# Issuing the first slab's store as two DMAs, the first in 4 KB and the second in 28 KB descriptors

One core of a Trainium2 (trn2) chip. The metric is the device time of one execution in microseconds (us).

## The reference

Rotary position embedding with heads split: `x` is 16 x 512 x 1024 float32 (33.55 MB), the output has the same size, and the two tables are small.

```python
x = x.reshape(batch, seq, num_heads, head_dim)
x1, x2 = x[..., :half_dim], x[..., half_dim:]
rotated = np.concatenate([x1 * cos - x2 * sin,
                          x1 * sin + x2 * cos], axis=-1)
```

## The kernel before

`x` is handled in 8 slabs of 4 MB, each as 128 partitions x 8 rows x 1024 elements; a partition's 32 KB are contiguous in DRAM. There are five slab buffers (`slots`), so load 5 has to wait for store 0, load 6 for store 1 and load 7 for store 2. Loads are issued on SP, stores on ACT. ACT casts a slab to bf16, DVE does two multiplications and an addition, and ACT casts back into the slab. The first slab and the last two are done in two halves of four rows.

```python
def load(s):
    slab[s] = slabs.tile([P, W], f32, tag="slab", name="slab")
    return nc.sync.dma_start(out=slab[s], in_=dram(x, s))
...
for s in range(nslabs):
    n = rpp if 1 <= s < nslabs - 2 else rpp // 2
    passes += [(s, r, n) for r in range(0, rpp, n)]

cast(passes[0])
for i, (s, r, n) in enumerate(passes):
    if i + 1 < len(passes):
        cast(passes[i + 1])
    ...                                    # two tensor_mul, one tensor_add on DVE
    nc.scalar.copy(out=xs, in_=xu)
    if r + n == rpp:
        nc.scalar.dma_start(out=dram(out_flat, s), in_=slab[s])
        if s + slots < nslabs:
            load(s + slots)
```

Of the kernel before, what the change touches and what calls it, by code (L numbers as in the profile page):

```python
# [2 lines left out]

# [4 lines left out]


@with_exitstack  # L10
def kernel(
    ctx: ExitStack,
    tc: tile.TileContext,
    x: bass.AP,
    cos: bass.AP,
    sin: bass.AP,
    num_heads: int,
    out: bass.AP,
):
    nc = tc.nc  # L20
    P = nc.NUM_PARTITIONS

    batch, seq, dim = x.shape
    nh = num_heads
    hd = dim // nh
    half = hd // 2
    bf16 = mybir.dt.bfloat16
    f32 = mybir.dt.float32

    nb = 2  # L30
    slots = 5
    nslabs = batch // nb
    rpp = nb * seq // P
    W = rpp * dim
    SP = seq // rpp
    TW = rpp * half

    out_flat = out.rearrange("b s h d -> b s (h d)")

    singles = ctx.enter_context(tc.tile_pool(name="singles", bufs=1))  # L40
    slabs = ctx.enter_context(tc.tile_pool(name="slabs", bufs=slots))
    xpool = ctx.enter_context(tc.tile_pool(name="xpool", bufs=2))
    psum = ctx.enter_context(tc.tile_pool(
        name="psum", bufs=1, space=bass.MemoryType.PSUM))


    def dram(t, s, a=0, n=W):
        return bass.AP(tensor=t.tensor, offset=t.offset + s * nb * seq * dim + a,
                       ap=[[W, P], [1, n]])


    def view(t, offset, *dims):
        return dataclasses.replace(t, offset=t.offset + offset,
                                   ap=[t.ap[0], *[list(d) for d in dims]])


    slab = {}
# [7 lines that stand above are left out]
    load(0)  # L65


    TR = seq // P
    G = rpp // TR
    table = {}  # L70
    raw = singles.tile([P, 2 * TR * half], f32, tag="raw")
    for i, src in enumerate((cos, sin)):
        table[i] = nc.gpsimd.dma_start(out=view(raw, i * TR * half, (1, TR * half)), in_=bass.AP(  # L73
            tensor=src.tensor, offset=src.offset,
            ap=[[TR * half, P], [1, TR * half]]))



    for s in range(1, slots):
        tc.add_manual_dep(  # L80
            load(s).ins, table[0].ins.name,
            mybir.DependencyInfo(mybir.DependencyClass.Sync,
                                 mybir.DependencyReason.DATA),
            reason="issue")



    pick = singles.tile([P, 2 * G * P], bf16, tag="pick")
    nc.gpsimd.memset(pick, 0.0)  # L89
    for g in range(2 * G):  # L90
        part = view(pick, g * P, (SP, P // SP), (1, SP))
        nc.gpsimd.affine_select(  # L92
            out=part, in_=part, compare_op=mybir.AluOpType.not_equal,
            fill=1.0 if g < G else -1.0, base=-(g % G),
            pattern=[[0, P // SP], [-G, SP]], channel_multiplier=1)

    tab1 = singles.tile([P, 2 * TR * half], bf16, tag="tab1")
    nc.gpsimd.tensor_copy(out=tab1, in_=raw)  # L98

    acc = psum.tile([P, 2 * rpp * hd], f32, tag="acc")  # L100
    for i in range(2):
        for h in range(2):
            for g in range(G):
                nc.tensor.matmul(  # L104
                    view(acc, (i * rpp + g * TR) * hd + h * half, (hd, TR), (1, half)),
                    view(pick, (i * h * G + g) * P, (1, P)),
                    view(tab1, i * TR * half, (half, TR), (1, half)),
                    start=True, stop=True)
    tab = singles.tile([P, 2 * rpp * hd], bf16, tag="tab")
    nc.vector.tensor_copy(out=tab, in_=acc)  # L110

    xb = {}


    def cast(u):
        s, r, n = u
        if r == 0:
            xb[s] = xpool.tile([P, W], bf16, tag="xb", name="xb")
        nc.scalar.copy(out=view(xb[s], r * dim, (1, n * dim)),  # L119
                       in_=view(slab[s], r * dim, (1, n * dim)))  # L120




    passes = []
# [9 lines that stand above are left out]
        xs = view(slab[s], r * dim, (1, n * dim))  # L135
        xu = view(xb[s], r * dim, (1, n * dim))

        t2 = view(slab[s].bitcast(bf16), 2 * r * dim, (1, n * dim))
        for t, a in ((t2, rpp * hd), (xu, 0)):
            nc.vector.tensor_mul(  # L140
                out=t, in0=xu,
                in1=view(tab, a + r * hd, (hd, n), (0, nh), (1, hd)))
        nc.vector.tensor_add(  # L143
            out=xu, in0=xu, in1=view(t2, half, (hd, n * nh), (-half, 2), (1, half)))

        nc.scalar.copy(out=xs, in_=xu)  # L146
        if r + n == rpp:
            nc.scalar.dma_start(out=dram(out_flat, s), in_=slab[s])
            if s + slots < nslabs:
                load(s + slots)  # L150


# [1 line left out]
_INS = ['x', 'cos', 'sin', 'num_heads']  # L154
_OUTS = [((16, 512, 16, 64), 'float32')]

_NUMBERS = {'num_heads': 16}


# [26 lines left out]
```

## Time and profile before

| | before |
|---|---|
| time, first chip, median of 4 runs | 162.02 us (161.98 to 162.12) |
| span of the profiled run | 160.4 us |
| bytes moved, mean rate | 67.24 MB, 419 GB/s |
| busiest compute engine | ACT, 71% |
| last store issued, landed | 145.28, 14.2 us later |

The page's own lines stand in the prediction below, with how to read them. In short: the DMA engines are full nearly all the time and no other engine is. One line more, from the view of the loads (minimum, median and maximum of the time from issue to landing); the maximum is load 4:

```profile
DMA to landing us min/median/max: 12.6/24.5/55.3
```

### The profile page before, as it was taken

The page shows a single profiled execution, that of the slowest core. Times are in us where ns is not written, and L with a number is a line of the kernel's source. Part 1 is how long each engine was busy: PE and PEld are TensorE (multiplying, and loading weights), DVE is VectorE, ACT ScalarE, POOL GpSimd, SP SyncE. Part 2 cuts the span into 40 slices and gives each one's busy share as a digit, 9 for nine tenths or more (in the row PEclk, how much of TensorE's full clock was granted, in tenths as well). Part 3 has the DMA queues.
Part 4 walks back from the last instruction along what each step waited for, and adds up shares of the span by engine and source line. Part 5 has one row for each costly group of instructions (what it writes and reads, how often), then busy time and mean ns, then how long its engine had stood idle before and what let it go on. Part 6 is the DMA issues. An engine that isn't in the chain of part 4 may idle for free.

```text
span 160.4 us, 169 instructions
## 1 busy us (share of the span) xinstructions
PE 1.0 (1%) x8; PEld 0.8 (1%) x8; DVE 108.5 (68%) x34; ACT 113.5 (71%) x23; POOL 3.4 (2%) x12
## 2 busy tenths in 40 slices
PE   0011000000000000000000000000000000000000
PEld 0010000000000000000000000000000000000000
DVE  0003799999989979997996099939749599930000
ACT  3006939998998999899907997099995999462000
POOL 7000000000000000000000000000000000000000
DMA  7999999999999999999999999999999999999995
GB/s 245 425 409 409 474 425 400 466 441 392 384 400 400 507 400 400 466 441 392 441 474 392 433 482 392 425 482 400 400 507 400 400 474 433 392 449 466 392 433 221
DMA packets 2368, 67.24 MB, mean 419 GB/s; under 512 B 288, under 2 KB 288, under 8 KB 320
## 3 DMA queue, kind: packets, MB, share of 16 engines
q1 hardware_dynamic: 1152, 33.55, 49.5%
q10 hardware_dynamic: 1152, 33.55, 48.4%
q0 software_dynamic: 64, 0.13, 0.2%
HBM read 33.69 MB, written 33.55 MB: 419 GB/s over the span
## 4 chain that ended last, share of the span: by engine, by line
DMA 59%; ACT 17%; issue 9%; DVE 4%; SPq 0%; ACTq 0%; POOLq 0%
DMA slab<-in_x_dram 39%; DMA out_dram<-slab 15%; ACT slab L146 11%; ACT xb L119 6%; DMA raw<-in_cos_dram 4%; DVE xb L140 1%; DVE xb L143 1%; DVE slab L140 1%; SPq L62 0%; ACTq L146 0%; POOLq L167 0%
## 5 line engine op out<-in xcount | busy, mean ns | idle before, releaser
L119 ACT CAST xb<-slab 128x4096 bf16<-128x4096 f32 (+1 forms) x11 | 56.6, 5155 | 27.5 <-DMA slab<-in_x_dram 26.2
L146 ACT CAST slab<-xb 128x4096 f32<-128x4096 bf16 (+1 forms) x11 | 56.6, 5153 | 3.5 <-DVE xb L143 3.5
L140 DVE TENSOR_TENSOR slab<-xb,tab 128x4096 bf16<-128x4096 bf16 (+1 forms) x11 | 35.9, 3260 | 19.9 <-ACT xb L119 19.8
L140 DVE TENSOR_TENSOR xb<-xb,tab 128x4096 bf16<-128x4096 bf16 (+1 forms) x11 | 35.9, 3261 | 0.3
L143 DVE TENSOR_TENSOR xb<-xb,slab 128x4096 bf16<-128x4096 bf16 (+1 forms) x11 | 35.9, 3261 | 0.3
L110 DVE CAST tab<-acc 128x1024 bf16<-128x1024 f32 x1 | 1.2, 1225 | 12.5 <-PE acc L104 12.5
L119 ACT ACT_TABLE_LOAD x1 | 1.3, 1283 | 0.7 <-PEq L167 0.7
L104 PE MATMUL acc<-tab,pick 128*128 128x128 bf16 x8 | 1.0, 305 | 11.5 <-POOL tab L98 11.5
L92 POOL TENSOR_SCALAR_AFFINE_SELECT pick<-pick 128x128 bf16<-128x128 bf16 x4 | 1.0, 288 | 0.1
L104 PEld LDWEIGHTS <-pick 128*128 128x128 bf16 x8 | 0.8, 136 | 11.4 <-issue 8.0
L73 POOL DMA_DIRECT2D raw<-in_cos_dram x1 | 0.7, 674 | 0.8 <-POOLq L167 0.8
L89 POOL MEMSET pick<- 128x512 bf16 x1 | 0.5, 543 | 0.0
L98 POOL CAST tab<-raw 128x256 bf16<-128x256 f32 x1 | 0.4, 396 | 6.9 <-DMA raw<-in_sin_dram 6.9
L73 POOL DMA_DIRECT2D raw<-in_sin_dram x1 | 0.5, 534 | 0.0
L167 POOL MEMSET const-float32-0.0<- 128x1 f32 x1 | 0.1, 99 | 0.2 <-issue 0.2
L167 POOL MEMSET const-bfloat16-1.0<- 128x1 bf16 x1 | 0.1, 102 | 0.0
L167 POOL MEMSET const-uint8-127<- 128x1 uint8 x1 | 0.1, 102 | 0.0
L167 POOL MEMSET const-float32-1.0<- 128x1 f32 x1 | 0.1, 99 | 0.0
## 6 DMA issues: line engine op xcount, KB each, us to landing
slab<-in_x_dram SPq DMA_DIRECT2D x8, 4096.0 KB, 24.5
out_dram<-slab ACTq DMA_DIRECT2D x8, 4096.0 KB, 26.6
raw<-in_cos_dram POOLq DMA_DIRECT2D x1, 64.0 KB, 7.0
raw<-in_sin_dram POOLq DMA_DIRECT2D x1, 64.0 KB, 9.0
```

Source lines behind the costliest of these rows:

```text
L73: table[i] = nc.gpsimd.dma_start(out=view(raw, i * TR * half, (1, TR * half)), in_=bass.AP(tensor=src.tensor, offset=src.offset, ap=[[TR * ...
L89: nc.gpsimd.memset(pick, 0.0)
L92: nc.gpsimd.affine_select(out=part, in_=part, compare_op=mybir.AluOpType.not_equal, fill=1.0 if g < G else -1.0, base=-(g % G), pattern=[[ ...
L98: nc.gpsimd.tensor_copy(out=tab1, in_=raw)
L104: nc.tensor.matmul(view(acc, (i * rpp + g * TR) * hd + h * half, (hd, TR), (1, half)), view(pick, (i * h * G + g) * P, (1, P)), view(tab1, ...
L110: nc.vector.tensor_copy(out=tab, in_=acc)
L119: nc.scalar.copy(out=view(xb[s], r * dim, (1, n * dim)), in_=view(slab[s], r * dim, (1, n * dim)))
L140: nc.vector.tensor_mul(out=t, in0=xu, in1=view(tab, a + r * hd, (hd, n), (0, nh), (1, hd)))
L143: nc.vector.tensor_add(out=xu, in0=xu, in1=view(t2, half, (hd, n * nh), (-half, 2), (1, half)))
L146: nc.scalar.copy(out=xs, in_=xu)
L167: nc = _bacc.Bacc("TRN2", target_bir_lowering=False, num_devices=1)
```

## The change

Its form suggests an intent: with short packets ahead, the first store should give way to the loads still under way. Only slab 0's store is touched.

```diff
-            nc.scalar.dma_start(out=dram(out_flat, s), in_=slab[s])
+            cuts = (0, dim, W) if s == 0 else (0, W)
+            for a, b in zip(cuts, cuts[1:]):
+                nc.scalar.dma_start(out=dram(out_flat, s, a, b - a),
+                                    in_=view(slab[s], a, (1, b - a)))
```

## The prediction

> **What bounds the kernel now.** I read the page's busy shares first, then the DMA rows, then the traffic in stretches of time, and the chain of waits last.
>
> ```profile
> span 160.4 us, 169 instructions
> PE 1.0 (1%) x8; PEld 0.8 (1%) x8; DVE 108.5 (68%) x34; ACT 113.5 (71%) x23; POOL 3.4 (2%) x12
> DMA  7999999999999999999999999999999999999995
> DMA packets 2368, 67.24 MB, mean 419 GB/s; under 512 B 288, under 2 KB 288, under 8 KB 320
> q1 hardware_dynamic: 1152, 33.55, 49.5%
> q10 hardware_dynamic: 1152, 33.55, 48.4%
> ```
>
> No compute engine is above 71%, while the 16 DMA engines are at 90% or more in every slice but the first and the last. The loads run in q1, the stores in q10; 1152 packets are 8 slabs times (128 rows of 32 KB + 16 completion packets), so one packet is one 32 KB row of a partition, 8 per DMA engine and slab. The next view gives stretches of time: start and end, length, busy times of the five engines, clock, DMA share, GB/s.
>
> ```profile
> 5.00:37.00 32.00, 1.01 (x8) 0.74 (x7) 21.16 (x9) 21.06 (x5) 0.40 (x1) 1.00 1.00 432
> 37.00:49.00 12.00, 0.00 (x0) 0.00 (x0) 11.15 (x3) 11.55 (x3) 0.00 (x0) 1.00 1.02 407
> 49.00:123.00 74.00, 0.00 (x0) 0.00 (x0) 59.88 (x17) 61.82 (x11) 0.00 (x0) 1.00 1.00 433
> 123.00:157.00 34.00, 0.00 (x0) 0.00 (x0) 16.31 (x8) 17.83 (x5) 0.00 (x0) 1.00 1.00 432
> ```
>
> Loads alone (5 to 37), loads and stores mixed (49 to 123) and stores alone (123 to 157) all run at 432 to 433 GB/s. There is one dip, where the first store joins the loads: 12 us x (1 - 407/432) = 0.7 us lost. 67.24 MB at 432 GB/s are 155.6 us of the 160.4 span. Of the other 4.8 us, 0.7 are this dip and the rest is start-up and the end. So the bound is DMA bytes, and an order of transfers can win only the dip.
>
> Two durations of packets. In the stretch from 130 to 158 us the store queue alone had 402 packets, 33 of them completions, at 100% of 16 engines: 28 x 16 / 369 = 1.21 us for 32 KB. In the stretch from 4 to 12 us:
>
> ```profile
> DMA packets 162, 3.34 MB, mean 418 GB/s; under 512 B 32, under 2 KB 32, under 8 KB 64
> q0 software_dynamic: 64, 0.13, 4.2%
> ```
>
> These are the tables, 32 packets of 4 KB and 32 completions: 4.2% of 8 us x 16 is 5.4 us, or about 0.16 us for a 4 KB packet with its share of the completion. An eighth of 1.21 us would be 0.152.
>
> Last, the dates (timeline of the issues and the copies, with the idle time before and its releaser):
>
> ```profile
> 37.11 0.38 ACTq L148 DMA_DIRECT2D out_dram<-slab  x1
> 66.23 7.02 ACT L119 CAST xb<-slab 128x8192 bf16<-128x8192 f32 x1 [0.41 <-ACT slab L146]
> 85.22 7.02 ACT L119 CAST xb<-slab 128x8192 bf16<-128x8192 f32 x1 [5.05 <-DMA slab<-in_x_dram]
> 123.96 3.61 ACT L119 CAST xb<-slab 128x4096 bf16<-128x4096 f32 x1 [1.83 <-DMA slab<-in_x_dram]
> 145.28 0.34 ACTq L148 DMA_DIRECT2D out_dram<-slab  x1
> ```
>
> Slab 0's store is issued at 37.11 and lands 24.4 us later, at 61.5. Load 5 reuses its slot and is issued at 61.59. Slab 4's cast (66.23) waits for ACT's own work, not for its load; those of slabs 5 (85.22) and 7 (123.96) wait for loads. The last store is issued at 145.28 and lands in 14.2 us, mostly queued behind store 6.
>
> **What the Trainium skill says.** "DMA: Bandwidth & Descriptors", section "Queues, rings and completion order": each DMA engine takes turns between its queues by whole packets, whatever their size. The trace agrees: between 65 and 84 us q1 had 142 packets and q10 143. The section's typical packet of 9 to 17 descriptors does not fit here, where one row is one packet. Section "Where 436 GB/s comes from" puts the ceiling at 435 GB/s; the trace has 432. Section "Why small descriptors are slow" gives about 3 cycles on top of one per 32 bytes: 3 on 128 for 4 KB, 2.3%; the trace's 0.16 against 0.152 us is some 5%, on so few packets that it costs nothing. "Perfetto Trace Analysis", section "DMA Optimizations", says that a split can help if DMA engines are generally idle; here they are not.
>
> **The change part by part.** Added: one DMA issue on ACT, about 0.38 us as the one at 37.11, at the price of a later cast of slab 2. ACT then has 5.05 us of idle time ahead of slab 5's cast, so this is absorbed. Added packets: 128 of 4 KB and 16 completions, per engine 8 x (0.16 - 0.152) = 0.06 us. Load 5 now waits for two stores instead of one; the order of instructions on every engine is otherwise the same, and the other shifted semaphore waits are on transfers that landed long before.
>
> What really moves is the sharing. From 41 us (37.11 plus the 3.8 us or so until store packets appear) an engine has 8 store packets of slab 0, some 1.5 load packets of slab 3 and 8 of slab 4 to move. Before, they alternate one to one, and both slabs take about the same time. After, a 4 KB store packet buys the load queue a whole 32 KB packet: 8 turns of 1.21 + 0.16 = 1.37 us, 11 us in all, in which the loads have 89% of the bandwidth. Then 1 to 2 load packets remain, against 28 KB packets (1.06 us): load 4 lands at about 41 + 11 + 1.5 x 1.21 + 1.06 = 55 instead of 64.9 (issued at 9.61, the longest landing, 55.3 us). Nobody waits for it: slab 4's cast stays at 66.2, so these 10 us are worth nothing.
>
> Store 0, on the other hand, now comes after all of load 4. Before, load 4 landed 3.4 us after store 0, with half of the traffic in that gap its own: 1.7 us at most of load work moves ahead of store 0, 1.2 if the store's completion no longer has to wait out a load packet. So store 0 lands 1.2 to 1.7 us later, load 5 is issued at 62.8 to 63.3, and the load queue is empty from 55 until then. The DMA engines don't idle: the rest of store 0 and store 1 (issued at 51.5) fill them. A load that joins a running store queue needs at most what store 0 needed to join the loads, 3.8 us, so it starts by 66.6 to 67.1; before, it followed load 4 at about 65.4. If it joins faster, it may even start earlier. I take load 5 to land 1.0 us later (from -0.5 to +1.7). Loads 6 and 7 stay back to back behind it: load 6 was issued at 79.7, some 5 us before load 5 landed, and load 7 at 99.0, again 5 us ahead. So casts 5 and 7 come about 1.0 us later, and the last store is issued at about 146.3.
>
> The end: a slab on idle engines lands 12.6 us after its issue (load 0), so the last store has 14.2 - 12.6 = 1.6 us of slack in its queue. 1.0 us fits. The sum for the time: no bytes change, +0.06 us of small packets, and 0 to 0.7 us if load 5's joining an empty queue repeats the dip of the first joining; half of that, 0.35. The dip itself may shrink with 4 KB packets, about -0.1. In all +0.3: 162.07 + 0.3 = 162.4.
>
> **The rivals.** First, the delay of load 5 goes through to the end: if it is over 1.6 us, the engines idle before the last store. With +1.7 and a repeated dip, 0.1 + 0.7 = 0.8 us, so about 162.9; were load 5 to join much more slowly, by 3 us, some 164. Against it: slack is seen in the backlog at 123 to 157, which runs at 432 without a hole. Second, the dip at 41 us goes away, because short packets let the store join softly: -0.7, so 161.4. For it speaks only that the dip is there and is the sole loss in mid-run. Third, the eight 4 KB descriptors of an engine are put into one packet: then the turns are as before and nothing moves, 162.1. Fourth, an earlier load 4 speeds the compute: against it is slab 4's cast, which waited for ACT. Even so the byte bound would keep the end where it is. A gain of over 2% (3.2 us) would need 0.7 us of dip and 2.5 us out of start-up that the change does not touch.
>
> **Range and chances.** 162.4, from 161.4 (the dip gone) to 163.5 (delay beyond the slack and a dip more). Faster by over 2% 0.01, within 2% 0.96, slower by over 2% 0.03.
>
> **What would show it.** 2512 packets in all, 1296 in q10, under 8 KB 464. Load 4 landing at about 45 us after issue instead of 55.3; store 0's second part landing at 62.7 to 63.2, load 5 issued right after it; GB/s at 430 or more from 49 to 157 us, with the load queue silent between about 55 and 66; slab 4's cast within 0.5 us of 66.2; slab 5's cast at about 86.2; the last store landing in about 13.2 us. I am wrong if the stretch after 123 us has a hole (first rival), if the stretch from 37 to 49 rises to 430 (second), or if load 4 still lands at 55 us after its issue (third).

## The result and the profile after

The changed kernel took 162.27 us (median of 4 runs, 162.07 to 162.49) against 162.02. The ratio is 1.0015, 95% interval 0.9997 to 1.0032: the same. (A ratio is the mean time of one kernel's runs over that of the other's of the same rounds, so not quite the ratio of the medians quoted.) A second series of 6 runs on another chip, told of below, gave 162.40 against 162.18, ratio 1.0011 (0.9992 to 1.0030).

The page of the changed kernel:

```profile
span 160.6 us, 173 instructions
PE 1.0 (1%) x8; PEld 0.8 (1%) x8; DVE 108.5 (68%) x34; ACT 113.5 (71%) x23; POOL 3.4 (2%) x12
DMA packets 2512, 67.24 MB, mean 419 GB/s; under 512 B 304, under 2 KB 304, under 8 KB 464
q1 hardware_dynamic: 1152, 33.55, 49.2%
q10 hardware_dynamic: 1296, 33.56, 48.4%
```

Packets are as predicted, 144 more in q10: every 4 KB descriptor is a packet of its own. Bytes, rate and busy times are those of before. The traffic in the same stretches of time:

```profile
5.00:37.00 32.00, 1.01 (x8) 0.74 (x7) 21.13 (x9) 21.04 (x5) 0.40 (x1) 1.00 1.01 434
37.00:49.00 12.00, 0.00 (x0) 0.00 (x0) 11.19 (x3) 11.59 (x3) 0.00 (x0) 1.00 0.99 409
49.00:123.00 74.00, 0.00 (x0) 0.00 (x0) 58.49 (x16) 61.30 (x11) 0.00 (x0) 1.00 1.00 432
123.00:157.00 34.00, 0.00 (x0) 0.00 (x0) 17.70 (x8) 18.34 (x6) 0.00 (x0) 1.00 1.00 432
```

No hole anywhere, and by these lines the dip from 37 to 49 us is 409 instead of 407 GB/s. That comparison hides something. The view counts a packet whole at its start, and one 32 KB packet on each of 16 engines, 0.5 MB, is 44 GB/s over 12 us. Shorter stretches, read as GB/s over DMA share (the second last figure), allow for that. Of the kernel before:

```profile
37.00:47.00 10.00, 0.00 (x0) 0.00 (x0) 9.15 (x3) 9.55 (x3) 0.00 (x0) 1.00 0.99 387
47.00:58.00 11.00, 0.00 (x0) 0.00 (x0) 10.86 (x3) 10.59 (x2) 0.00 (x0) 1.00 0.99 429
```

and of the changed one:

```profile
37.00:47.00 10.00, 0.00 (x0) 0.00 (x0) 9.20 (x3) 9.59 (x3) 0.00 (x0) 1.00 1.03 439
47.00:58.00 11.00, 0.00 (x0) 0.00 (x0) 10.84 (x3) 10.59 (x2) 0.00 (x0) 1.00 0.96 397
```

387/0.99 = 391 and 433 GB/s before, 426 and 414 after: the dip has moved to where the 28 KB packets begin, and it is smaller. In the trace's record of single packets (start, duration, size), 24 load packets that started between 39.0 and 42.5 us took over 1.4 us before, up to 2.25 instead of the usual 1.21; over 1.21 us that adds up to 0.90 us for each of the 16 engines. In the changed kernel 16 did from 47.6 us on and two when load 5 joined, 0.45 us for each engine. Over all profiles this sum is 0.45 to 0.78 us in the five with 4 KB packets first, and 0.70 to 0.90 in the six with store 0 in one DMA, so how much the dip shrinks varies.

Underneath, the order of the transfers is another, too. The queues between 56 and 66 us (packets, MB, share of 16 engines' time), of the kernel before:

```profile
q10 hardware_dynamic: 86, 2.29, 53.2%
q1 hardware_dynamic: 82, 2.16, 50.1%
```

and of the changed one:

```profile
q10 hardware_dynamic: 159, 4.36, 101.0%
q1 hardware_dynamic: 17, 0.03, 0.8%
```

The load queue is silent in that stretch, and the stores take all of it. The dates in the changed kernel's timeline, and the landing of its loads:

```profile
33.63 3.85 ACTq L151 DMA_DIRECT2D out_dram<-slab  x2
66.21 7.02 ACT L119 CAST xb<-slab 128x8192 bf16<-128x8192 f32 x1 [0.41 <-ACT slab L146]
86.61 7.02 ACT L119 CAST xb<-slab 128x8192 bf16<-128x8192 f32 x1 [6.46 <-DMA slab<-in_x_dram]
125.33 3.61 ACT L119 CAST xb<-slab 128x4096 bf16<-128x4096 f32 x1 [1.82 <-DMA slab<-in_x_dram]
146.65 0.34 ACTq L151 DMA_DIRECT2D out_dram<-slab  x1
```

```profile
DMA to landing us min/median/max: 12.6/25.8/49.8
```

Load 4 lands 5.5 us earlier (49.8 against 55.3 us after an issue at 9.62), and slab 4's cast stays at 66.2, as it waited for ACT. Slab 5's cast is 1.39 us later (86.61 against 85.22), slab 7's 1.37, the last store's issue 1.37. In the record of single packets the last store's last completion is at 159.15, against 159.17 before: the 1.4 us of delay are gone by the end. That is the slowest engine. The last store has 16 completion packets, one from each engine; their median came at 158.47 instead of 158.88 (158.65 in the second series' profile), so most engines finished earlier, by about as much as the dip shrank, and the slowest did not. What the span is longer by, 0.2 us, comes after that. SP's last drains, of the kernel before (count; shortest, median and longest ns; first and last start):

```profile
L181 SPq DRAIN  x3: 7/7/7, 159.6 to 159.9; - x3
```

and of the changed one:

```profile
L185 SPq DRAIN  x3: 7/7/7, 159.8 to 160.1; - x3
```

In the trace SP waits at the end for the completions of the DMAs issued from SP and ACT, in a fixed order of eight counters, which the DMAs use over and over. Before, there are 16 DMAs, and the last one uses the counter that is waited for last. With 17, the last store uses the first counter, and when it has landed four waits are still to be gone through, at 159.535, 159.600, 159.661 and 159.720 us: 0.06 us each.

### The profile page after: what moved, and what is told of

It reads as the page before. It is cut to its first block, busy times and chain, and to the rows that moved or that the text cites. A ratio compares the mean times of both kernels' runs of the same rounds, so it can differ in the third digit from the quotient of the medians.

```text
span 160.6 us, 173 instructions
## 1 busy us (share of the span) xinstructions
PE 1.0 (1%) x8; PEld 0.8 (1%) x8; DVE 108.5 (68%) x34; ACT 113.5 (71%) x23; POOL 3.4 (2%) x12
## 2 busy tenths in 40 slices
DMA packets 2512, 67.24 MB, mean 419 GB/s; under 512 B 304, under 2 KB 304, under 8 KB 464
## 3 DMA queue, kind: packets, MB, share of 16 engines
q10 hardware_dynamic: 1296, 33.56, 48.4%
## 4 chain that ended last, share of the span: by engine, by line
DMA 51%; ACT 30%; issue 6%; DVE 4%; ACTq 0%; SPq 0%; POOLq 0%
DMA slab<-in_x_dram 26%; DMA out_dram<-slab 20%; ACT slab L146 16%; ACT xb L119 14%; DMA raw<-in_cos_dram 4%; DVE slab L140 1%; DVE xb L143 1%; DVE xb L140 1%; ACTq L151 0%; SPq L62 0%; ACTq L146 0%; POOLq L171 0%
## 5 line engine op out<-in xcount | busy, mean ns | idle before, releaser
L110 DVE CAST tab<-acc 128x1024 bf16<-128x1024 f32 x1 | 1.2, 1225 | 12.5 <-PE acc L104 12.5
L104 PEld LDWEIGHTS <-pick 128*128 128x128 bf16 x8 | 0.8, 136 | 11.4 <-issue 8.0
## 6 DMA issues: line engine op xcount, KB each, us to landing
out_dram<-slab ACTq DMA_DIRECT2D x1, 3584.0 KB, 25.5
```

The source lines that it names most:

```text
L104: nc.tensor.matmul(view(acc, (i * rpp + g * TR) * hd + h * half, (hd, TR), (1, half)), view(pick, (i * h * G + g) * P, (1, P)), view(tab1, ...
L110: nc.vector.tensor_copy(out=tab, in_=acc)
```

## The experiments

My theories after the result: (a) DMA engines take turns by packets, so a 4 KB packet buys the loads a 32 KB one; (b) what the loads win early nobody needs, and the delay of load 5 is taken up by the backlog ahead of the last store, so the bytes set the time; (c) the 0.2 us are waits at the end of the program. Rivals stand with each run. Twelve kernels ran, on other chips than the first; the kernel before took 162.24 there (medians of 11 and 9 runs) and 162.18 (11 runs).

### late_split: the same split where only stores move

```diff
-            cuts = (0, dim, W) if s == 0 else (0, W)
+            cuts = (0, dim, W) if s == 5 else (0, W)
```

> The same split (4 KB rows, then 28 KB rows) on slab 5's store instead of slab 0's, where only stores are moving. Theory 'end of the program': the changed kernel's 0.2 us come from the waits that SP does one after the other at the end; with 17 instead of 16 DMAs from SP and ACT the last store's completion is met before four other waits instead of after them. Then this kernel, which also has 17, is 0.2 us slower than before too (162.2 to 162.3), and its profile shows about 0.2 us more between the last landing and the end of the span. Rival 'early traffic': the 0.2 us come from the sharing between store 0 and loads 3 and 4, which is untouched here: then 162.0.

162.42 us (162.34 to 162.75), ratio 1.0013 (1.0001 to 1.0025). Load 5 landed no later than in the kernel before (84.1 by its last packet, 84.9 there), and the drains stand as in the changed kernel:

```profile
L185 SPq DRAIN  x3: 7/7/7, 159.8 to 160.1; - x3
```

So 0.2 us appear without any change to the early traffic. The time from the last completion to the end of the span agrees in all profiles: 1.21 to 1.23 us in four kernels with 16 DMAs, 1.43 to 1.46 in the seven profiles with 17, 1.59 in the one with 19, where six waits follow, and 1.21 to 1.22 in the two with 24, where the last store is again on the last counter. Theory (c) is shown.

### lane7 and late_pieces: back to the last counter

```diff
-            cuts = (0, dim, W) if s == 0 else (0, W)
+            cuts = {0: (0, dim, W), 5: (0, 4 * dim, 6 * dim, W), 6: (0, 4 * dim, 6 * dim, W),
+                    7: (0, 2 * dim, 4 * dim, 6 * dim, W)}.get(s, (0, W))
```

> The changed kernel, with the late stores 5, 6 and 7 in 3, 3 and 4 pieces so that there are 24 DMAs and the last store's completion is again the last that SP waits for. No piece changes the sharing with loads: stores are alone by then. Theory 'end of the program': back to 162.0, or a little under it, with load 5 still landing at about 86.2. Rival 'early traffic': stays at 162.2 to 162.3.

162.93 us (162.32 to 163.49, in two groups: 162.3 to 162.6 and 163.3 to 163.5), ratio 1.0040 (1.0015 to 1.0064). The tail is back to 1.21 us as expected, but the time is not: in the profiled run one engine's last completion came at 160.45, the median engine's at 158.95. The control has the late pieces and a whole store 0:

```diff
+            cuts = {5: (0, 2 * dim, 4 * dim, 6 * dim, W), 6: (0, 4 * dim, 6 * dim, W),
+                    7: (0, 2 * dim, 4 * dim, 6 * dim, W)}.get(s, (0, W))
```

> Control for the kernel with 24 DMAs: slab 0's store is whole again and the late stores 5, 6 and 7 are in 4, 3 and 4 pieces, which makes 24 DMAs as well. Theory 'late pieces cost nothing, the spread comes from the early part': time of the kernel before, 162.0 to 162.5 in every run, with 0.4 us from the last landing to the last drain. Rival 'the pieces cost time or upset the engines': 162.5 to 163.5 as the kernel with 24 DMAs had.

162.51 us (162.45 to 162.71), ratio 1.0018 (1.0004 to 1.0032), just over what I expected: the pieces cost some 0.3 us themselves, so lane7 was no clean test of the time. By themselves they don't cause the second group, which none of late_pieces' five runs shows.

### row7_first: the 4 KB part from the second half

```diff
-            cuts = (0, dim, W) if s == 0 else (0, W)
-            for a, b in zip(cuts, cuts[1:]):
+            cuts = ((W - dim, W), (0, W - dim)) if s == 0 else ((0, W),)
+            for a, b in cuts:
```

> The split taken from the other end: first row 7 in 4 KB descriptors, then rows 0 to 6 in 28 KB descriptors. Row 7 is written by slab 0's second copy, so both parts are issued at about 37.1 us, as the prediction assumed for the first part (it was 33.6). Theory 'one packet a turn': first store packets at about 41, slab 4's load lands 45 to 47 us after its issue (49.8 in the changed kernel, 55.3 in the kernel before), store 0 lands at 62.3 all the same, load 5 starts at the same time; time as the changed kernel, 162.1 to 162.4. Rival 'bytes are shared evenly, packet size is of no account': slab 4's load lands at about 55 us after issue.

162.63 us (162.18 to 163.07, two runs at each end), ratio 1.0030 (1.0008 to 1.0052), over the 162.1 to 162.4 that I expected. Both parts were issued at 37.2 and 37.6 us, and the loads landed so:

```profile
DMA to landing us min/median/max: 12.7/25.8/46.6
```

46.6 us is within the 45 to 47 expected. The packets alternate as theory (a) has it, and my figure of 45 failed mainly on the date at which they start: 3.2 of the 4.8 us between 49.8 and 45.

### by_partition: two DMAs, no short packet

The edit is against the kernel before.

```diff
-            nc.scalar.dma_start(out=dram(out_flat, s), in_=slab[s])
+            d, t = dram(out_flat, s), slab[s]
+            for p, n in ((0, 16), (16, 112)) if s == 0 else ((0, P),):
+                nc.scalar.dma_start(
+                    out=bass.AP(tensor=d.tensor, offset=d.offset + p * W, ap=[[W, n], [1, W]]),
+                    in_=t[p:p + n, :])
```

> Slab 0's store in two DMAs of the same 512 KB and 3.5 MB, but cut by partitions: 16 rows of 32 KB, then 112 rows of 32 KB; no packet is smaller. Theory 'one packet a turn': the sharing is that of the kernel before: slab 4's load lands about 55 us after issue, load 5 is issued at about 61.5, slab 5's cast is at about 85.2. Rival 'the split itself, two DMAs in place of one, gives the loads way': landing near 50. Time: 17 DMAs, so 162.2 by the theory 'end of the program'.

```profile
DMA to landing us min/median/max: 12.9/27.4/55.6
```

Load 4 lands at 55.6: two DMAs alone give the loads no way, the packets' size does. But the time, 165.54 us (165.34 to 166.03), ratio 1.0206 (1.0190 to 1.0223), is a miss. Store 0 landed late, load 5 was issued at 65.35 instead of 61.4 to 61.6, and the last store at 151.34. The traffic from 37 us on:

```profile
37.00:49.00 12.00, 0.00 (x0) 0.00 (x0) 10.70 (x3) 11.08 (x3) 0.00 (x0) 1.00 1.01 371
49.00:123.00 74.00, 0.00 (x0) 0.00 (x0) 56.31 (x15) 57.70 (x10) 0.00 (x0) 1.00 1.00 427
```

371 and 427 GB/s against 407 and 433 are about 1.0 and 1.0 us of traffic lost. In the record of single packets it sits in 32 store packets between 41.7 and 69.3 us that took up to 4.4 us, 2.1 us for each engine; in the kernel before none took over 1.22. Why this cut slows them stays open. The time then follows: the last store was issued 6.1 us later than before and landed 11.1 us after, so that 6.1 less the slack of 3.1 us (measured in late_load7 below) goes through. The last completion came at 162.10, 2.9 us later, and the waits at the end add 0.25 us.

### halves: 16 KB packets

```diff
-            cuts = (0, dim, W) if s == 0 else (0, W)
+            cuts = (0, 4 * dim, W) if s == 0 else (0, W)
```

> Slab 0's store in two halves of 16 KB descriptors. The first half is issued at 33.6 as in the changed kernel. Theory 'one packet a turn': from 37 us a turn of 16 KB and 32 KB takes 1.21 + 0.61 = 1.82 us; 13.5 load packets are left, so slab 4's load lands at 37 + 13.5 x 1.82 = 61.6, 52 us after its issue, between 49.8 (4 KB) and 55.3 (32 KB); store 0 lands at 62.3 again. Time 162.1 to 162.6. Rival 'two DMAs give the loads way, whatever their packets': 49 to 50 us.

```profile
DMA to landing us min/median/max: 12.7/25.4/50.9
```

50.9 us, between 49.8 (4 KB) and 55.3 (32 KB), but nearer the rival's 49 to 50 than my 52: I had put 13.5 load packets where the changed kernel's trace leaves about 12.5. By itself this run does not part the theories; by_partition does. The time, 162.15 us (162.12 to 162.33), ratio 0.9998 (0.9980 to 1.0016), is the best of all variants, and equal to the kernel before. Its last completion came at 158.91, 0.26 us earlier than there, with 0.44 us of slow load packets instead of 0.90; the longer wait at the end (1.44 against 1.21 us) takes that back.

### small_last: the 28 KB part first

```diff
-            cuts = (0, dim, W) if s == 0 else (0, W)
+            cuts = (0, W - dim, W) if s == 0 else (0, W)
```

> The order of the two parts turned round: rows 0 to 6 in 28 KB descriptors first, row 7 in 4 KB descriptors last. Theory 'one packet a turn': store 0 alternates with the loads nearly as before until about 59, then its last 8 short packets let what is left of load 4 by: load 4 lands at about 62 (52 us after issue), store 0's last part at 62 to 63, load 5 is issued about 1 us later than before, slab 5's cast at 85.2 to 86.6. Time 162.1 to 162.4 (17 DMAs). Rival 'the early lead of load 4 counts for something': differs from the changed kernel by more than 0.3 us.

Load 4 landed 52.5 us after its issue and load 5 was issued at 63.2: the sharing is as expected. The time is 163.39 us (162.76 to 163.66), ratio 1.0058 (1.0035 to 1.0081), over my 162.1 to 162.4 and apart from the changed kernel, as the rival said, though not for the rival's reason: slab 5's load landed as late as in the changed kernel. In the stretch after 159.2 us the DMA queue still shows:

```profile
DMA packets 3, 0.03 MB, mean 23 GB/s; under 512 B 2, under 2 KB 2, under 8 KB 2
q10 hardware_dynamic: 3, 0.03, 5.5%
```

One packet of 32 KB and two completions. 5.5% of 1.4 us x 16 is 1.2 us, one packet on one engine, while the other 15 are done. The mean rate does not show this; the slowest engine sets the end.

### split_012: the split on all three stores that loads wait for

```diff
-            cuts = (0, dim, W) if s == 0 else (0, W)
+            cuts = (0, dim, W) if s < 3 else (0, W)
```

> The split on the stores of slabs 0, 1 and 2, whose slots loads 5, 6 and 7 reuse. Theory 'one packet a turn, with slack of 1.6 us at the end': store 1's 4 KB packets go out in the hole of the load queue and change nothing; store 2's give loads 5 and 6 way, so store 2 lands about 103 instead of 97.4, load 6 lands well before and the load queue has a second hole; load 7 lands at about 126 to 127 instead of 124.95, the last store is issued at 147.8 to 148.5 and lands 12 to 12.6 us later: 160.0 to 161.0 in the trace against 159.5, so 162.6 to 163.5. Rival 'the end is bytes alone, any order is absorbed': 162.2.

163.14 us (162.51 to 163.66), ratio 1.0053 (1.0025 to 1.0082), inside the range, but by another road. Load 7 landed at 125.5 and the last store was issued at 147.2, yet its median engine was done at 158.57, between the changed kernel's two profiles (158.47 and 158.65), and its slowest at 159.40. In the profiled run 0.4 of the 0.6 us over the first profile come from the tail of 1.59 us and the rest from the slowest engine, none from used-up slack.

### late_load7 and late_load5: how much delay is free

Both edits are against the kernel before and shortened here. Load 7 waits for slab 5's last vector instruction, and in the second kernel load 5 for one of slab 3's and two memsets, with loads 6 and 7 issued behind it. No store is split.

```diff
+        if s == nslabs - 3 and r + n == rpp:          # late_load7: add is slab 5's tensor_add
+            tc.add_manual_dep(load(nslabs - 1).ins, add.ins.name, ...)
```

> The kernel before, with load 7 made to wait for slab 5's last vector instruction (ends at 105.6) instead of being issued at 99.0. It starts 3 to 5 us later than before. Theory 'slack of 1.6 us': the last store is issued 3 to 5 us later and the time rises by 1.5 to 3.5 us, 163.5 to 165.5, with a hole in the DMA traffic ahead of the last store. Rival 'the last store is behind a backlog that absorbs it': 162.0 to 162.3. Rival 'no slack at all': 165 to 167.

163.79 us (163.12 to 163.98), ratio 1.0088 (1.0066 to 1.0110). The last store was issued at 149.38, 4.1 us later than before. The rate from 145 to 157 us is 393 GB/s, which is the hole, and the store with nothing ahead of it lands in the minimum of this line:

```profile
145.00:157.00 12.00, 0.00 (x0) 0.00 (x0) 0.66 (x1) 3.60 (x1) 0.00 (x0) 1.00 0.92 393
DMA to landing us min/median/max: 11.1/26.9/33.2
```

So a free store takes 11.1 us, and the slack before is 14.2 - 11.1 = 3.1 us, not the 1.6 that I had taken from load 0. The last completion came at 160.12, 0.96 later: 4.1 less 3.1 is 1.0. The profiled run was the fastest; the other three took 0.6 to 0.9 us more, which this sum does not explain. So 163.79 lies in the range of my theory although its slack of 1.6 us was wrong.

```diff
+            if s == 3 and a:                          # late_load5: mul is slab 3's first tensor_mul
+                late = nc.gpsimd.memset(pick, 0.0)    # waits for mul
+                late = nc.gpsimd.memset(pick, 0.0)
+                tc.add_manual_dep(load(slots).ins, late.ins.name, ...)
```

> No split at all: the kernel before, with load 5 made to wait for a vector instruction of slab 3 and two memsets behind it, so that it is issued at about 64.7 instead of 61.6 and the load queue runs empty for 2 to 3 us. The last store is issued 2 to 3 us later, inside the 3.1 us of slack that two runs have shown. Theory 'a load that joins an empty queue beside running stores makes an engine fall behind': the runs spread up to 163.5 as those of the split kernels do, with one engine's last store a packet late. Rival 'the 4 KB packets do that': time of the kernel before, 162.0 to 162.5 in every run.

162.31 us (162.18 to 162.57), ratio 1.0006 (0.9991 to 1.0020). Slab 5's cast was at 88.19, 3.0 us later than before, and the last store's issue at 148.24, 3.0 later; it landed 11.4 us after, at 159.6 against 159.5. Twice the delay of the changed kernel costs nothing: theory (b) is shown. The run also takes down the theory that a load joining an empty queue throws an engine back: there is no second group here.

### drop_row: 512 KB less

```diff
-            nc.scalar.dma_start(out=dram(out_flat, s), in_=slab[s])
+            a = dim if s == 3 else 0
+            nc.scalar.dma_start(out=dram(out_flat, s, a, W - a), in_=view(slab[s], a, (1, W - a)))
```

> Wrong on purpose: the kernel before, whose store of slab 3 leaves out row 0 of each partition (512 KB of 67.24 MB). Theory 'bytes are the bound': 0.524 MB at 432 GB/s, 1.21 us less, all of it at the end as the last store has 1.6 us of slack: 160.8. Rival 'the chain from load 7 to the last store is the bound': 162.0 to at most 0.3 less.

160.87 us (160.71 to 160.91) against 162.24, ratio 0.9914 (0.9902 to 0.9926). The output lacks a row, as intended. 1.37 us less by the medians, 1.21 expected: bytes are the bound.

### after_again: the changed kernel once more

No edit.

> The changed kernel unaltered, beside the others. Theory 'end of the program plus an engine that falls behind': in this batch's terms, 0.2 us over the kernel before from the waits at the end in every run, and in some runs up to 1.2 us more, in which one of the 16 DMA engines finishes its last store one packet after the others: runs spread from about 162.2 to 163.5. Rival 'only the waits at the end': all runs 0.1 to 0.4 over the kernel before.

162.40 us (162.04 to 163.04), ratio 1.0011 (0.9992 to 1.0030). Five of six runs are within 0.4 us of the kernel before's median, one is 0.9 over: some spread, not up to 163.5.

The spread taken together: the kernels with 4 KB packets beside loads (both series of the changed kernel, lane7, row7_first, small_last, split_012) have runs that lie 0.4 to 1.2 us apart, in five of the six some 0.9 or more; late_split, late_pieces, halves, late_load5 and drop_row, without them, 0.2 to 0.4. But by_partition and late_load7, without them too, have 0.7 and 0.9; their last store came after the slack was used up. The kernel before, in far more runs, spans 0.4 to 0.6 in a series. So among the kernels that stay within the slack, the wider spread goes with 4 KB packets beside loads; with four to six runs of each, that is a hint and not shown. One engine a packet behind is seen in the profile of small_last, and a last engine 1.5 us after the median in that of lane7. The lag is there long before the end: in small_last the first and the last engine finish store 4 2.0 us apart (129.4 and 131.4 us), as they do the last store; in the kernel before it is 0.6 us both times. How it comes to that, no run shows.

## Why the prediction was right, and where not

- **Bytes are the bound.** Right: drop_row takes the time of its bytes off, and no order of transfers beat the kernel before. That an order can win only the dip held as well: halves won 0.26 us of it and lost them to the waits at the end.
- **A 4 KB packet buys the loads a 32 KB one.** Right in kind: by_partition has no lead, row7_first a landing at 46.6. Wrong in the date. I let the first part be issued at 37.1 with the rest, but it needs row 0 alone, which the first half's copy had written: it was issued at 33.63. Its eight turns began some 4 us earlier and were spent in part on load 3, so load 4 landed at 59.4 and not at 55, and the queue was silent from 59 and not from 55 us. The order of the instructions had not changed; what each of them waits for had.
- **Nobody waits for load 4.** Right: slab 4's cast stayed at 66.2.
- **Store 0 lands 1.2 to 1.7 us later, load 5 about 1.0.** Right: the second part, issued at 37.13, landed 25.5 us later, at 62.7 against 61.5. Load 5's first packet started at 66.6, 3.8 us after its issue, as assumed. Slab 5's cast moved by 1.39, within -0.5 to 1.7.
- **The slack takes it up.** Right in kind, mis-sized: 3.1 us instead of 1.6. Load 0, from which I took the time of a free transfer, needed 12.6 us at the cold start; a free store needs 11.1.
- **The sum.** I put +0.06 for small packets, +0.35 for half a second dip and -0.1 for a smaller first one. By the packet record the small packets took the 0.159 us each that I had put, the second dip is 0.04 us instead of 0.35 (two slow load packets), and the first dip, 0.90 and not the 0.7 that the stretch showed, fell to 0.45, by 0.45 instead of 0.1. These terms together give a gain of some 0.35 us, and the median engine did end 0.4 us earlier. The slowest engine did not, and why is open. What makes the span longer, 0.2 us, is a term that the prediction lacks: the waits at the end. So +0.3 came close to the measured 0.25, itself within the noise, by luck: the terms were others.
- **The rivals.** The first (delay beyond the slack) is what late_load7 makes and the change does not. The second (no dip) came half true: no load packet took over 1.4 us while the 4 KB packets ran, but the dip came back with the 28 KB packets, at half the size, and the time did not fall. The third (descriptors packed together) failed at 1296 packets. The fourth (an earlier load 4 speeds the compute) failed at slab 4's cast.

## What to carry to other kernels

In this kernel, where the DMA engines are full from start to end, moving the order of transfers gave a lead to some and took it from others. With equal bytes, the end moved by more than 1 us only where a transfer came so late that the engines ran dry (late_load7, by_partition) or, in small_last, one engine was a packet behind. So measure that slack on a transfer with nothing ahead of it, in the same phase. A DMA that covers part of a tile can be issued as soon as that part is written, so ask what each new piece waits for, not only where it stands. And at differences of 0.1%, look at what the program does after the last byte, and at the slowest of the DMA engines instead of their mean.

## What the Trainium skill lacked or had wrong

- "DMA: Bandwidth & Descriptors", section "Queues, rings and completion order": the typical packet of 9 to 17 descriptors was not seen for DMAs issued from SP and ACT. Each descriptor of 4, 28 and 32 KB was a packet of its own (2512 packets, 144 more than before), so the size of a descriptor sets a queue's share: load 4 landed after 49.8 us with 4 KB packets against it and 55.3 with 32 KB.
- The pages that I read do not have these: SP's waits at the end, about 0.06 us for each that still follows the last landing (1.21, 1.44 and 1.59 us from it to the end of the span with 16, 17 and 19 DMAs); a loss where stores first join loads, 0.70 to 0.90 us for each engine with 32 KB store packets (load packets of up to 2.25 us instead of 1.21 in the kernel before) and 0.45 to 0.78 with 4 KB packets ahead; and a DMA engine that falls behind while loads and stores mix and stays behind (2.0 us between the first and the last engine in small_last, at store 4 and at the end).
